# Two-layer attention encoder: the last pair's output stays in SBUF, the output projection loads two tiles ahead, and the last pair and the first transfers are reordered

## The chip, the cores and the metric

One core of one Trainium2 chip runs the whole kernel in one launch. The metric is the device time of that launch in microseconds (us), shown as the median of several runs; a separate profiled execution gives the trace.

## The reference

1088 tokens (1024 of a prompt, 64 of a sample that has 256 cached positions) go through two layers of width 1024. Cut to what matters:

```python
# layer 0: one input projection feeds two groups of 8 heads, one output projection
q_a, ckv, kr, q_b, k_b, v_b = _even_project(x, pos, w_in, g_q, w_uq, g_kv)   # latents, RMS norm, rotation
o_a = _blockwise(lambda qb, pb: _softmax_attend(qb, k_a, v_a, _chunk_mask(pb, pos), MLA_SCALE), q_a, pos)
o_b = _band_prompt(q_b, k_b, v_b, table)
y = jnp.concatenate([o_a.reshape(B, S, H_A * V_DIM), o_b.reshape(B, S, H_B * HEAD_DIM)], -1) @ w_out
# layer 1: 16 stick-breaking heads
log_1m = jnp.where(mask, jax.nn.log_sigmoid(-z), 0.0)
tail = lax.cumsum(log_1m, axis=z.ndim - 1, reverse=True) - log_1m
w = jnp.where(mask, jnp.exp(jax.nn.log_sigmoid(z) + tail), 0.0)
return o.reshape(B, S, MIX_C) @ w_out, k, v
# both layers
x = _layer_norm(ALPHA * x + mix, g1, b1)
ff = jnp.square(jax.nn.relu(x @ w_up)) @ w_down
return _layer_norm(ALPHA * x + ff, g2, b2)
```

The change touches the latents of layer 0 (`x @ w_in` for the first 1056 columns) and `y = concat(...) @ w_out` with the layer norm behind it, in both layers.

## The kernel before

Everything is fp32. A product of two fp32 matrices is done as three matmuls on TensorE (`mm3`): each operand is split into a high half H, which ScalarE writes, and a low half L = x - H, which VectorE writes (`split`); the products are H*H, H*L and L*H. So each operand passes ScalarE and VectorE before TensorE can use it. Tokens come in nine tiles of 128 (`TOK`, the last of 64).

The order of instructions on each engine is set by a planner that runs when the kernel is built, from the order in which the code issues them; TensorE, ScalarE, VectorE and GpSimd then execute their own rows in order, and all DMAs are issued in order from SyncE's queue. A row waits for the data that it reads and for the readers of the buffer that it overwrites; all behind it on the same engine waits too.

- `latents` (the start): the weight columns for the key latent (`w_ck`, four pieces), x (nine tiles, `xraw`) and the columns for the query latent (`w_ql`, eight pieces) are loaded and split; nine tiles of key latents, then nine of query latents are made. GpSimd rotates part of each key tile (`ropem`). g_q, the query constants (`qconst`, spread into a DRAM buffer `qr_d`) and the first weights of the head pairs (`w_bk`, `w_bq`, `w_bv`) are loaded here too.
- `attend`: a pair of heads has nine units (head, quarter; quarter 4 is the sample's), done in the order `self.order`. Each unit's output `o` goes to DRAM: to `oT_d`, seven blocks of 128 rows of the concatenated heads, or, for the pair that comes last (`self.late`), to `oTl_d`.
- `out_early`: while the last pair's attention still runs, w_out's eight blocks are loaded and split, and three tiles of tokens in layer 0 (`EARLY`: 0, 4, 1; four in layer 1: 0, 4, 1, 5) are multiplied with the seven blocks that are ready. `self.paced` interleaves these steps with the units.
- `out_proj`: then, in the order `OUT_ORDER`, the rest: an early tile needs only the late block's product, any other tile all eight. `operand` loads a tile's rows of `oT_d` and `oTl_d`, splits them and loads the residual. A layer norm (`norm`) follows each tile; the last two tiles run together.
- Buffers of one size, called slots, are shared by w_out, operands, residuals and results (`Slots`: `take` gives the first free one that fits, `give` puts it at the end of the list). A tile's name in a listing, as `wo0_10_2136`, is the slot (`wo0_10`) and a running number. Whoever takes a slot waits for the last reader of what was in it.

Line numbers in the profile: 138 and 139 are the two halves of `split`, 143 to 145 the matmuls of `mm3`, 161 a transpose, 304, 309 and 318 the loads of w_ck, w_ql and x, 169 the load of a weight, 607 and 609 the scans of the stick-breaking attention, 674 and 676 the products with V, 1043 and 1044 the loads of an operand.

## Time and profile before

| | |
|---|---|
| median of 3 runs | 2840.68 us (2839.82 to 2844.84) |
| profiled execution | 2842.44 us, of which 2840.6 are the span of the trace |
| mean granted TensorE clock | 0.987 |
| TensorE busy (PE) | 2737.7 us, 96% |
| VectorE (DVE), ScalarE (ACT), GpSimd (POOL) busy | 76%, 53%, 27% |
| DMA | 335.60 MB, 118 GB/s in the mean |

The page names lines of the program and tiles without their numbers: `s<-xH,wH` is a product of xH and wH into the PSUM tile s. "[1.52 <-ACT sl L138]" behind an instruction is the idle time of its engine before it, and what ended that. The chain is the row of work that ended last, followed back from the end. A window row gives, after the stretch and its length, the busy time of PE, PEld, DVE, ACT and POOL in it (with the number of instructions), the clock that was granted to TensorE, the mean busy share of the DMA engines and the GB/s moved.

### The profile page before, as it was taken

The page shows a single profiled execution, that of the slowest core. Times are in us where ns is not written, and L with a number is a line of the kernel's source. Part 1 is how long each engine was busy: PE and PEld are TensorE (multiplying, and loading weights), DVE is VectorE, ACT ScalarE, POOL GpSimd, SP SyncE. Part 2 cuts the span into 40 slices and gives each one's busy share as a digit, 9 for nine tenths or more (in the row PEclk, how much of TensorE's full clock was granted, in tenths as well). Part 3 has the DMA queues.
Part 4 walks back from the last instruction along what each step waited for, and adds up shares of the span by engine and source line. Part 5 has one row for each costly group of instructions (what it writes and reads, how often), then busy time and mean ns, then how long its engine had stood idle before and what let it go on. Part 6 is the DMA issues. An engine that isn't in the chain of part 4 may idle for free.

```text
span 2840.6 us, 46995 instructions
## 1 busy us (share of the span) xinstructions
PE 2737.7 (96%) x16907; PEld 2499.6 (88%) x16907; DVE 2160.4 (76%) x3837; ACT 1512.2 (53%) x3104; POOL 776.0 (27%) x890
## 2 busy tenths in 40 slices
PE   7999989999999999999999999998999999999998
PEld 7999978887899998878789999998879999977776
DVE  4266684885867777999978888888686777689998
ACT  4266664882555556333247777777445555543331
POOL 3123341652200002222533344344230000122235
PEclk9999999999999999999999999998999999999999
DMA  7122155334243447344231111113242444654442
GB/s 225 51 77 76 56 152 151 84 109 147 98 136 129 148 159 267 118 145 143 82 110 57 46 60 51 51 53 103 78 144 86 159 141 136 230 177 133 158 122 77
DMA packets 235752, 335.60 MB, mean 118 GB/s; under 512 B 45472, under 2 KB 168128, under 8 KB 235520
## 3 DMA queue, kind: packets, MB, share of 16 engines
q1 hardware_dynamic: 235520, 332.61, 37.2%
q8 instruction: 134, 2.20, 0.3%
q14 instruction: 98, 0.80, 0.1%
HBM read 217.83 MB, written 113.33 MB: 117 GB/s over the span
## 4 chain that ended last, share of the span: by engine, by line
PE 78%; DVE 9%; ACT 4%; DMA 4%; issue 3%; POOL 1%; SPq 0%; DVEq 0%; ACTq 0%; POOLq 0%
PE d L143 9%; PE d L144 9%; PE d L145 9%; PE s L143 5%; PE s L145 5%; PE s L144 5%; PE t L143 5%; PE t L144 5%; PE t L145 5%; PE t L161 4%; PE s L542 3%; PE pv L676 2%; PE pv L674 2%; PE pv L145 2%; PE pv L143 2%
## 5 line engine op out<-in xcount | busy, mean ns | idle before, releaser
L610 POOL TENSOR_TENSOR G<-G,S 128x384 f32<-128x384 f32 (+4 forms) x200 | 207.4, 1041 | 347.8 <-DVE S L607 128.4
L143 PE MATMUL d<-xH,wH 128*128 128x384 f32 (+1 forms) x792 | 266.4, 336 | 1.7 <-ACT kraw L509 1.6
L145 PE MATMUL d<-xH,wL 128*128 128x384 f32 (+1 forms) x792 | 264.0, 333 | 1.6 <-DVE wL L139 1.6
L144 PE MATMUL d<-xL,wH 128*128 128x384 f32 (+1 forms) x792 | 264.0, 333 | 0.0
L139 DVE TENSOR_TENSOR wtL<-t,wtH 128x512 fp32r<-128x512 f32 (+2 forms) x328 | 196.8, 618 | 54.3 <-ACT wtH L138 47.1
L138 ACT ACTIVATE wtH<-t 128x512 fp32r<-128x512 f32 (+2 forms) x328 | 170.6, 545 | 64.4 <-PE t L161 32.8
L549 POOL TENSOR_TENSOR R<-R,inv 128x640 f32<-128x640 f32 (+6 forms) x100 | 118.7, 1195 | 185.5 <-DVE inv L548 117.6
L674 PE MATMUL pv<-wtH,V 128*128 128x256 f32 (+1 forms) x624 | 159.3, 280 | 8.3 <-ACT o L634 4.0
L676 PE MATMUL pv<-wtL,V 128*128 128x256 f32 (+1 forms) x624 | 155.2, 289 | 7.0 <-DVE wtL L139 7.0
L143 PEld LDWEIGHTS d<-xH,wH 128*128 128x128 f32 x792 | 150.1, 190 | 5.4 <-ACT kraw L509 2.7
L607 DVE TENSOR_TENSOR_SCAN S<-S,own 128x513 f32<-128x513 f32 (+3 forms) x144 | 143.9, 1006 | 13.8 <-ACT S L600 12.2
L145 PEld LDWEIGHTS d<-xH,wL 128*128 128x128 f32 x792 | 149.9, 189 | 3.2 <-DVE wL L139 1.8
L144 PEld LDWEIGHTS d<-xL,wH 128*128 128x128 f32 x792 | 149.9, 189 | 1.0
L138 ACT ACTIVATE wo<-wo 128x1024 fp32r<-128x1024 f32 (+4 forms) x100 | 87.9, 883 | 113.9 <-DMA wo<-a_d 21.4
L674 PEld LDWEIGHTS pv<-wtH,V 128*128 128x128 f32 x624 | 120.1, 192 | 13.7 <-ACT o L634 6.3
L676 PEld LDWEIGHTS pv<-wtL,V 128*128 128x128 f32 x624 | 120.0, 192 | 10.8 <-DVE wtL L139 9.6
L161 PE MATMUL t<-ident,G 128*128 128x128 f32 x600 | 107.4, 282 | 12.6 <-POOL G L610 6.4
L542 PE MATMUL s<-kS,qH 128*128 128x384 f32 (+3 forms) x288 | 106.4, 372 | 4.9 <-ACT G L601 2.7
L600 ACT ACTIVATE S<-s 128x384 f32<-128x384 f32 (+4 forms) x200 | 99.1, 495 | 12.3 <-PE s L542 8.7
L601 ACT ACTIVATE G<-s 128x384 f32<-128x384 f32 (+4 forms) x200 | 100.1, 501 | 0.7 <-PE t L161 0.7
L139 DVE TENSOR_TENSOR wo<-wo,wo 128x1024 fp32r<-128x1024 f32 (+3 forms) x72 | 81.9, 1140 | 24.2 <-ACT wo L138 24.2
L542 PE MATMUL s<-kS,qL 128*128 128x384 f32 (+3 forms) x288 | 97.7, 341 | 0.0
(1724 smaller groups left out, 9836.0 us busy)
## 6 DMA issues: line engine op xcount, KB each, us to landing
wo<-a_d SPq DMA_DIRECT2D x53, 512.0 KB, 3.6
a_d<-wo SPq DMA_DIRECT2D x34, 544.0 KB, 4.2
sl<-a_d SPq DMA_DIRECT2D x29, 512.0 KB, 3.7
wo<-in_w_up SPq DMA_DIRECT2D x26, 512.0 KB, 4.1
wo<-in_w_dn SPq DMA_DIRECT2D x25, 512.0 KB, 5.4
sl<-in_w_dn SPq DMA_DIRECT2D x23, 512.0 KB, 6.3
xs<-a_d SPq DMA_DIRECT2D x19, 512.0 KB, 3.6
a_d<-sl SPq DMA_DIRECT2D x17, 544.0 KB, 5.0
```

The costliest lines, as they stand in the source:

```text
L138: self.nc.scalar.activation(H, src, AF.Copy)
L139: (engine or self.nc.vector).tensor_tensor(L, src, H.bitcast(F32), op=ALU.subtract)
L143: i = mm(out, aH, bH, start=first, stop=False)
L144: mm(out, aH, bL, start=False, stop=False)
L145: mm(out, aL, bH, start=False, stop=last)
L161: return self.nc.tensor.transpose(out, in_, self.ident[:n, :n])
L542: self.nc.tensor.matmul(ps[:, :n], q, k, start=i == 0, stop=i == len(passes) - 1)
L549: nc.gpsimd.tensor_tensor(R[:, :nk], R[:, :nk], inv.to_broadcast([P, nk]), op=ALU.mult)
L607: nc.vector.tensor_tensor_scan(s[r], s[r], own, carry, op0=ALU.mult, op1=ALU.max)
L610: nc.gpsimd.tensor_tensor(G[:, :n], G[:, :n], S[:, 1 : n + 1], op=ALU.mult)
L674: mm(out, v, wH[:, s : s + n], start=bi == 0 and s == 0, stop=False)
L676: mm(out, v, wL[:, s - n : s], start=False, stop=bi == len(banks) - 1 and j == bank[-1][0])
```

## The change

Four parts.

1. The start. `x_piece` runs two tiles ahead of the products and w_ql's pieces one tile later than before; the loads of g_q, the query constants, w_bk, w_bq and w_bv get a dependency without a wait (`after`) on a later product (`marks`), which moves them back in the planner's order.
2. The last pair of each layer has an order of units of its own (`LAST`), and its output goes by DMA from SBUF to SBUF into a slot, `late_raw`, instead of to `oTl_d`; `late_part` splits it in pieces of 256 tokens. An early tile then needs no load of its own.
3. `out_proj` loads operands ahead (`out_load` for the tile three places on, `out_operand` for the split of the one two places on, between the two halves of a tile's products). `OUT_ORDER` begins with tile 6, which is no early tile; its load stands at the start of the last early tile's step, its split at the end (`self.ahead`). g and b are loaded behind it, and `new_xq` is called there.
4. The slots are taken in another order: `out_space` adds the `wo` slots and takes `late_raw` before the five slots of the weight pool are put in the list.

How the rows move. First SyncE's queue at the start of the program (`praw` are pieces of w_ck and w_ql, `xraw` tiles of x, `wraw` weights, `qc` and `qr_d` the query constants). Before:

```order
L304 DMA praw_98<-in_w_ck 128x576
L318 DMA xraw_102<-in_xT 128x8x128
L304 DMA praw_106<-in_w_ck 128x576
L344 DMA rope_118<-in_rope_tok 128x288
L290 DMA gkv_120<-in_g_kv 128x256
L290 DMA gq_122<-in_g_q 128x768
L318 DMA xraw_181<-in_xT 128x8x128
L304 DMA praw_110<-in_w_ck 128x576
L169 DMA wraw_975<-in_w_bk 128x1024
L410 DMA qc_1363<-in_qconst 32x384
L318 DMA xraw_242<-in_xT 128x8x128
L304 DMA praw_114<-in_w_ck 128x576
```

And in the changed kernel, in the same place:

```order
L313 DMA praw_97<-in_w_ck 128x576
L327 DMA xraw_101<-in_xT 128x8x128
L313 DMA praw_105<-in_w_ck 128x576
L327 DMA xraw_117<-in_xT 128x8x128
L356 DMA rope_121<-in_rope_tok 128x288
L299 DMA gkv_123<-in_g_kv 128x256
L313 DMA praw_109<-in_w_ck 128x576
L327 DMA xraw_125<-in_xT 128x8x128
L313 DMA praw_113<-in_w_ck 128x576
L327 DMA xraw_182<-in_xT 128x8x128
L318 DMA praw_186<-in_w_ql 128x768
L327 DMA xraw_243<-in_xT 128x8x128
```

The second, third and later x tiles move ahead; g_q, w_bk and the query constants are gone from here. g_q stands at row 36 of the queue now, the constants at rows 52 to 60, w_bk, w_bq and w_bv at rows 63, 66 and 67.

Second, layer 0, where the last early tile ends and the first whole tile (6) begins: the changed kernel's ACT rows. `wo0_0_1888` is `late_raw`, `wo0_19_2161` the late block's high half, `xs0_7` the raw rows of tile 2, `wo0_1_2132` those of tile 6 and `wo0_10_2136` tile 6's high half.

```order
L646 ACTIVATE otmp_2088_8395<-pv_2083_8381 64x256
L647 ACTIVATE o_2087_8394<-pv_2083_8381 64x256
L141 ACTIVATE wo0_19_2161_8659<-wo0_0_1888_7781 128x256 x4
L141 ACTIVATE xs0_10_2199_8839<-xs0_7_2186_8766 128x896
L141 ACTIVATE wo0_10_2136_8617<-wo0_1_2132_8567 128x896
```

Behind the last output of the attention (`o_2087`) come the four pieces of the late block, one other tile's split and then tile 6's; before the change this place held a split of one 128x128 piece of the late block. The PE rows there:

```order
L146 MATMUL d_2135_8594<-wraw_2108_8438,wo0_16_2129_8562 128x512
L147 MATMUL d_2135_8594<-wH0_2109_8439,wo0_16_2129_8562 128x512
L148 MATMUL d_2135_8594<-wraw_2108_8438,wo0_19_2130_8563 128x512
L146 MATMUL s_2175_8681<-wo0_2_2090_8402,wo0_10_2136_8617 128x512
L147 MATMUL s_2175_8681<-wo0_3_2091_8403,wo0_10_2136_8617 128x512
```

The last early matmul reads slot `wo0_19`, into which the late block's high half goes next, and the row behind it already needs tile 6's high half, in slot `wo0_10`, which held the last early tile's residual until then. In layer 1 the places are alike: tile 6's first matmul follows the last early one, and on ACT four pieces of the late block and then tile 6's split stand between.

Third, VectorE in layer 1 ahead of the early products (`wo1_3`, `wo1_6` and so on, 128x1024, are low halves of w_out's blocks, `wtL` and `S` belong to the attention, 128x896 is the low half of the first early tile). Before:

```order
L139 TENSOR_TENSOR wo1_12_4919_23840<-wo1_10_4917_23837,wo1_11_4918_23839 128x1024
L139 TENSOR_TENSOR wtL_4751_23296<-t_4749_23290,wtH_4750_23295 128x512
L607 SCALAR_TENSOR_TENSOR S_4765_23355<-S_4765_23355,own_3390_16535 128x513
L139 TENSOR_TENSOR wo1_15_4922_23846<-wo1_13_4920_23843,wo1_14_4921_23845 128x1024
L607 SCALAR_TENSOR_TENSOR S_4776_23395<-S_4776_23395,own_3390_16535 128x385
L139 TENSOR_TENSOR wo1_18_4925_23852<-wo1_16_4923_23849,wo1_17_4924_23851 128x1024
L139 TENSOR_TENSOR wtL_4754_23309<-t_4752_23303,wtH_4753_23308 128x512
L139 TENSOR_TENSOR wtL_4757_23322<-t_4755_23316,wtH_4756_23321 128x512
L139 TENSOR_TENSOR wraw_4928_23858<-wo1_19_4926_23855,wo1_20_4927_23857 128x896
```

And now:

```order
L142 TENSOR_TENSOR wo1_12_4907_23831<-wo1_10_4905_23828,wo1_11_4906_23830 128x1024
L142 TENSOR_TENSOR wo1_7_4923_23863<-wL1_4920_23858,wo1_4_4922_23862 128x896
L620 SCALAR_TENSOR_TENSOR S_4785_23395<-S_4785_23395,own_3383_16529 128x385
L142 TENSOR_TENSOR wtL_4774_23352<-t_4772_23346,wtH_4773_23351 128x512
L142 TENSOR_TENSOR wo1_15_4910_23837<-wo1_13_4908_23834,wo1_14_4909_23836 128x1024
L142 TENSOR_TENSOR wo1_18_4913_23843<-wo1_16_4911_23840,wo1_17_4912_23842 128x1024
L142 TENSOR_TENSOR wtL_4777_23364<-t_4775_23359,wtH_4776_23363 128x384
L651 TENSOR_TENSOR o_4764_23321<-pv_4757_23295,o_4764_23321 64x256
L622 SCALAR_TENSOR_TENSOR S_4788_23405<-S_4788_23405,S_4785_23395 128x385
L142 TENSOR_TENSOR wraw_4916_23849<-wo1_19_4914_23846,wo1_20_4915_23848 128x1024
```

The early tile's low half (128x896) stood behind all of w_out's splits that this stretch holds; it now stands ahead of three of them.

The diff, cut to its core:

```diff
-OUT_ORDER = [[0, 5, 4, 2, 1, 6, 8, 3, 7], [0, 2, 4, 6, 1, 5, 8, 3, 7]]
+OUT_ORDER = [[6, 4, 5, 0, 2, 1, 8, 3, 7], [6, 4, 2, 0, 5, 1, 8, 3, 7]]
+LAST = [[(0, 3), (1, 1), (0, 2), (1, 0), (0, 4), (1, 3), (0, 1), (1, 2), (0, 0)],
+        [(0, 0), (1, 1), (0, 1), (1, 2), (0, 4), (1, 3), (0, 2), (0, 3), (1, 0)]]
...
+    def after(self, dma, mark):
+        if mark is not None:
+            self.tc.add_manual_dep(dma.ins, mark.ins.name, mybir.DependencyInfo(
+                mybir.DependencyClass.NoSync, mybir.DependencyReason.DATA), reason="pace")
...
+        marks = []
         ck_piece(0)
         x_piece(0)
         for k in (2, 4, 6):
             ck_piece(k)
+        x_piece(1)
         rope = self.tl(pa, [P, 9, ROPE], "rope", 1)
         nc.sync.dma_start(rope, io["rope_tok"])
         gkv = self.bcast(pa, io["g_kv"], CKV, "gkv")
-        gq = self.bcast(pa, io["g_q"], QL, "gq")
+        gq = None
 
         for t, (t0, n) in enumerate(TOK):
+            if t < 7:
+                x_piece(t + 2)
             if t:
-                x_piece(t)
-            if t < 8:
-                ql_piece(t)
+                ql_piece(t - 1)
...
+        gq = self.bcast(pa, io["g_q"], QL, "gq", marks[5])
...
-                first = self.weight(io["w_bk"][0], [P, KD, P])
+                first = self.weight(io["w_bk"][0], [P, KD, P], marks[-1])
...
-            nc.sync.dma_start(qc[:, :n], io["qconst"][:, c0 : c0 + n])
+            self.after(nc.sync.dma_start(qc[:, :n], io["qconst"][:, c0 : c0 + n]), marks[10])
...
-        return (self.oTl_d if blk == self.late else self.oT_d[blk - (blk > self.late)]), r
+        return (self.late_raw.bitcast(F32) if blk == self.late else self.oT_d[blk - (blk > self.late)]), r
...
+    def out_space(self, layer, side):
         sl = self.slots = Slots(self)
+        sl.add(f"wo{layer}", side, 21 if layer else 20, 0)
+        self.late_raw = sl.take([T], F32R)
+        self.order = LAST[layer]
         for tag in ("wraw", "wH0", "wL0", "wH1", "wL1"):
             sl.free.append((self.wp, tag, 0, D))
-        sl.add(f"wo{layer}", side, 21 if layer else 20, 0)
...
+                lhs[t] = self.out_operand(t, xres)
+                ys[t] = sl.take([D]), lhs[t].pop()
+                if t == EARLY[layer][-1]:
+                    self.ahead = self.out_load(OUT_ORDER[layer][0], xres)
...
+                    self.ahead = self.out_operand(OUT_ORDER[layer][0], xres, self.ahead)
...
+    def out_load(self, t, xres):
+        sl, (t0, n) = self.slots, TOK[t]
+        raw, xr = sl.take([KD, P]), sl.take([D])
+        self.nc.sync.dma_start(raw[:, : KD - 1, :n], self.oT_d[:, :, t0 : t0 + n].rearrange("k p t -> p k t"))
+        self.nc.sync.dma_start(xr[:n], xres[t0 : t0 + n, :])
+        return raw, xr
+    def out_operand(self, t, xres, loaded=None):
+        sl, (t0, n) = self.slots, TOK[t]
+        raw, xr = loaded or self.out_load(t, xres)
+        oH = sl.take([KD, P], F32R)
+        oL = sl.take([KD, P], F32R) if n == P else None
+        lo = oH[:, :, n:] if oL is None else oL
+        self.split(oH[:, : KD - 1, :n], lo[:, : KD - 1, :n], raw[:, : KD - 1, :n])
+        if oL is None:
+            self.split(oH[:, KD - 1, :n], lo[:, KD - 1, :n], self.late_raw[:, t0 : t0 + n].bitcast(F32))
+        sl.give(raw)
+        return [oH, oL, xr]
...
+        late = [sl.take([T], F32R), self.late_raw]
+        turned = set()
+        def late_part(t):
+            u = t // 2
+            if t < 8 and u not in turned:
+                turned.add(u)
+                c = slice(u * 2 * P, (u + 1) * 2 * P)
+                self.split(late[0][:, c], late[1][:, c], late[1][:, c].bitcast(F32))
+        loads, ops = {}, {order[0]: self.ahead}
+        def load(t):
+            if t is not None and t not in ys and t not in ops:
+                loads[t] = self.out_load(t, xres)
 
         def operand(t):
+            if t is None:
+                return
+            late_part(t)
+            if t in ys:
+                ops[t] = None, None, None
+            elif t not in ops:
+                ops[t] = self.out_operand(t, xres, loads.pop(t))
...
+        load(order[1])
+        load(order[2])
+        gb = [self.bcast(sl, io[f"ln_mix_{x}"][layer : layer + 1, :], D) for x in "gb"]
+        operand(order[0])
+        operand(order[1])
+        between[0]()
+        for j, t in enumerate(order[:-2]):
+            load(order[j + 3] if j + 3 < len(order) else None)
+            oH, oL, xr = ops[t]
+            if xr is not None:
+                ys[t] = sl.take([D])
+            early = oH is None
...
+                if h == 0:
+                    operand(order[j + 2])
```

More of the change, by code (lines that the diff above doesn't have):

```diff
@@ L1528, in do, with start @@
                 prep[c].pop(0)()
+        def start():
+            self.new_xq()
+            prep.extend(self.quadrant_sums(c) for c in range(2))
         def before():
@@ L1539, in after @@
             do(0, 1)
-        self.out_proj(layer, ws, ys, xres, xmid, (before, after))
+        self.out_proj(layer, ws, ys, xres, xmid, (start, before, after))
         plain(0, 0)
```

115 lines of the change are left out of this document (48 added, 67 removed).

## The prediction

> **What bounds the kernel now.** I read the page first, for who carries the end of the kernel. The first line is busy time by engine; the second is the share of each in the chain of work that ended last.
>
> ```profile
> PE 2737.7 (96%) x16907; PEld 2499.6 (88%) x16907; DVE 2160.4 (76%) x3837; ACT 1512.2 (53%) x3104; POOL 776.0 (27%) x890
> PE 78%; DVE 9%; ACT 4%; DMA 4%; issue 3%; POOL 1%; SPq 0%; DVEq 0%; ACTq 0%; POOLq 0%
> ```
>
> PE is busy for 2737.7 of 2840.6 us. The change neither adds nor removes a matmul (PE's matmuls in the two listings add up to the same number of columns), so all that can be won is the 2840.6 - 2737.7 = 103 us in which PE stands, and time in which it runs at half its clock. Next I read, by stretches, the three places that the change touches: the start, the step from layer 0's attention into its output projection, and the same step in layer 1. The columns are PE, PEld, DVE, ACT and POOL busy, granted clock, DMA share, GB/s.
>
> ```profile
> 20.00:30.00 10.00, 7.60 (x59) 7.36 (x58) 6.09 (x10) 6.63 (x18) 4.87 (x13) 1.00 1.07 374
> 30.00:40.00 10.00, 9.21 (x73) 8.95 (x71) 6.01 (x11) 6.88 (x19) 9.42 (x26) 1.00 0.97 278
> sum 70.00, PE 52.10 PEld 49.22 DVE 31.55 ACT 33.96 POOL 21.81; mean PE 7.44 PEld 7.03 DVE 4.51 ACT 4.85 POOL 3.12
> 660.00:670.00 10.00, 6.96 (x34) 5.22 (x32) 2.98 (x6) 1.07 (x3) 0.73 (x1) 1.00 0.44 121
> 670.00:680.00 10.00, 5.99 (x15) 4.53 (x16) 7.38 (x10) 4.54 (x6) 2.94 (x2) 0.66 1.04 327
> 1970.00:1980.00 10.00, 8.30 (x45) 6.22 (x44) 7.50 (x11) 8.53 (x19) 3.68 (x8) 0.84 0.83 295
> 1980.00:1990.00 10.00, 5.53 (x19) 3.76 (x18) 10.00 (x9) 9.42 (x18) 5.40 (x6) 0.50 0.76 248
> 1990.00:2000.00 10.00, 6.27 (x26) 5.87 (x26) 10.00 (x11) 5.04 (x10) 4.57 (x7) 0.50 0.21 69
> 2000.00:2010.00 10.00, 10.00 (x61) 8.79 (x60) 9.32 (x14) 5.05 (x14) 3.36 (x9) 0.97 0.34 97
> 2050.00:2060.00 10.00, 10.00 (x44) 7.86 (x43) 1.92 (x5) 1.37 (x2) 0.00 (x0) 1.00 0.96 300
> ```
>
> The sum row is of 0 to 70 us: PE stands 17.9 us there, all of it before 60. In 660 to 680 it stands 7.05 us, in 1970 to 2000 9.9 us, with a clock of 0.50 from 1980 on and DVE full. At 2050 to 2060, where layer 1's output projection begins, PE does not stand at all.
>
> **The start.** What PE waited for up to 62 us, and the chain in order of time:
>
> ```profile
> PE d L143 <- ACT xH L138: 7.2, 1, 7.2
> PE s L143 <- ACT xH L138: 3.3, 2, 2.7
> PE s L143 <- ACT wqlH L138: 2.9, 1, 2.9
> 6.33 8.69 DMA wraw<-in_w_bk
> 17.53 5.99 DMA wraw<-in_w_bq
> 47.08 3.90 DMA xraw<-in_xT
> 12.89 1.06 ACT L138 ACTIVATE xH<-xraw 128x1024 fp32r<-128x1024 f32 x1 [4.95 <-DMA xraw<-in_xT]
> ```
>
> PE waits for pieces of x and of the latent weights, and the chain to them runs through loads of w_bk and w_bq, which PE needs only much later. The last tile of x is issued at 47.08. The change takes gq, the query constants with their twelve stores into qr_d, w_bk, w_bq and w_bv out of this queue and puts them behind it, and moves each x tile two tiles ahead.
>
> What that can give at most: 17.9 us of standing, less the first 7.2 us, which stay (the first products still need the same first piece of w_ck and of x), leaves 10.7 us. To it come matmuls at half clock. In the next rows one of 288 columns follows the one before after 0.24 us until 17.3 us, and after 0.13 us then; some 22 of them, 0.11 us each, are 2.4 us.
>
> ```profile
> 9.14 0.44 PE L144 MATMUL d<-wckL,xH 128*128 128x288 f32 x1
> 9.38 0.44 PE L145 MATMUL d<-wckH,xL 128*128 128x288 f32 x1
> 17.71 0.29 PE L143 MATMUL s<-wckH,xH 128*128 128x288 f32 x1
> 17.84 0.29 PE L144 MATMUL d<-wckL,xH 128*128 128x288 f32 x1
> ```
>
> So 13 us is the ceiling. How much of it is reached follows from the loads. Per tile the new queue brings 524 KB of x and 393 KB of w_ql, 917 KB; at the 278 to 374 GB/s of the rows that takes 2.5 to 3.3 us, and the 24 matmuls of a tile at 0.13 us take 3.1 us. Loads and products are about even, so small waits stay, and POOL's chain for the key's rotation (9.42 of 10 us busy in 30 to 40) is not shortened. By bytes, w_bk, w_bq and w_bv (0.52 MB each), gq (0.39 MB) and the qr_d stores (12 of up to 0.20 MB) are 4.3 MB, 11.5 us at 374 GB/s, which agrees with the ceiling. I take 9 us, 4 to 12. Below 4 it would need POOL or the load of the last tile of x to hold PE as now. The work that was moved back costs nothing where it goes: after 60 us PE is full and the queues are nearly idle, and the first product with w_bk comes at 130 us:
>
> ```profile
> 100.00:110.00 10.00, 10.00 (x62) 9.97 (x61) 2.48 (x6) 2.04 (x6) 0.55 (x1) 1.00 0.14 39
> L143 PE MATMUL s<-xH,wH x32: 306/334/426, 130.8 to 159.3; 128*128 128x384 f32 x24, 128*128 128x320 f32 x8
> ```
>
> If this cover were gone, a weight would be late by its load and split, 6 to 9 us by the two rows of the chain.
>
> **Layer 0, entry into the output projection.** The last early tile's products are issued up to 665 us; then:
>
> ```profile
> 666.81 0.51 PE L143 MATMUL s<-wo,sl 128*128 128x512 f32 x1 [1.52 <-ACT sl L138]
> 674.01 0.79 PE L143 MATMUL s<-wH,xs 128*128 128x512 f32 x1 [5.53 <-ACT xs L138]
> 679.30 0.60 PE L143 MATMUL s<-wo,xs 128*128 128x512 f32 x1
> 679.73 0.41 PE L144 MATMUL s<-wo,xs 128*128 128x512 f32 x1
> 666.47 6.36 DMA xs<-oTl_d
> 672.91 1.06 ACT L138 ACTIVATE xs<-xs 128x1024 fp32r<-128x1024 f32 x1 [0.46 <-DMA xs<-oTl_d]
> ```
>
> First 1.52 us for the late block's reload, then 5.53 us for the first whole tile, whose load is issued only now, and behind that 13 matmuls at 0.43 us where 0.23 is normal, 2.6 us. Together 9.7 us. The change removes the reload, loads tile 6 before the last early tile and issues g and b behind. But it does not remove the stall. In the order of instructions (above, in the part on the change) tile 6's high half is written into the slot that held the residual of the last early tile, and the late block's high half into the slot of that tile's low half, which PE reads until its last early matmul. So behind that matmul ACT must do four late pieces of 128x256, then the next tile's split (it is ahead on the same queue), then tile 6's split, and only then does PE go on. Prices, from groups of the same shape:
>
> ```profile
> L138 ACT ACTIVATE wtH<-t 128x256 fp32r<-128x256 f32 x16 | 6.0, 378 | 6.4 <-PE pv L674 5.5 <-PE t L161 0.4 <-PE pv L691 0.4
> L138 ACT ACTIVATE wo<-wo 128x896 fp32r<-128x896 f32 x5 | 4.8, 957 | 1.7 <-DVE wH L1021 1.5 <-DMA wo<-oT_d 0.2
> ```
>
> 4 x 0.38 + 2 x 0.96 = 3.4 us, and 0.2 us of signals: 3.6. Whether half clock follows such a gap lies between two rows: behind 1.52 us the matmuls kept 0.23 us, behind 5.53 us they lost 2.6; I take 2. New loss 5.6, gain 9.7 - 5.6 = 4 us; bounds 1 (2.6 us lost and 2 us more, if the raw tile or the split ahead of it is late) and 9.7 (no stall). The Trainium skill ("TensorE: Matmul & The Clock Gate", Part 1) gives a window of about 3.4 us that runs freely, and half the clock after an idle one. By that rule 3.6 us of idle need not fill a window, the penalty could be nothing and the gain 6 us; no row here shows a gap of 3.6 us. The new order of the last pair's units does not change when the early products can start here, and one more split of w_out falls into that stretch, about 1 us of ACT, which I put within the bounds.
>
> **Layer 1.** The stretch before the early products:
>
> ```profile
> PE pv L676 <- DVE wtL L139: 4.2, 2, 3.2
> PE t L161 <- POOL G L610: 3.8, 2, 2.4
> 1991.50 1.20 DVE L139 TENSOR_TENSOR wo<-wo,wo 128x1024 fp32r<-128x1024 f32 x1
> 1992.62 1.84 DVE L607 TENSOR_TENSOR_SCAN S<-S,own 128x385 f32<-128x385 f32 x1
> 1996.70 1.08 DVE L139 TENSOR_TENSOR wraw<-wo,wo 128x896 fp32r<-128x896 f32 x1
> 2000.10 0.94 DVE L607 TENSOR_TENSOR_SCAN S<-S,own 128x385 f32<-128x385 f32 x1
> 2001.39 0.48 PE L143 MATMUL d<-wH,wo 128*128 128x512 f32 x1
> ```
>
> DVE is the bound: seven splits of w_out, the first tile's split, scans and attention splits stand in one row, and the first early product (2001.39) gives PE work of its own. Before, the first tile's low half comes behind all seven w_out splits; after, behind four or five, with the rest behind it. Between them and now one finds two splits of 1.2 us less, about two scans of 0.94 to 1.84 less and one attention split of about 0.6, so the first early product can start about 6 us earlier, at 1995, or a little more. But it needs the last weight blocks within its 21 matmuls (4.8 us at 0.23), and these two or three splits come only 4 to 7 us behind. Of some 21 us lost from 1971 to 2001 (9.9 standing, the rest at half clock) I take 7 as won, 0 to 12. Here the range is widest: the scans, 0.94 us alone and 1.84 us beside a busy POOL, make DVE's sum uncertain by some microseconds.
>
> At the projection's start the same new wait comes, where now there is none (10.00 of 10 us busy): four late pieces and tile 6's split, 4 x 0.38 + 0.96 + 0.2 = 2.7 us, and 0 to 2.6 us of half clock, of which I take 1.5. Sum for layer 1: 7 - 4.2 = 3 us, from -5 to 10.
>
> **The sum.** 9 + 4 + 3 = 16 us. The profiled execution took 2842.4 us (span 2840.6 and 1.8 around it), 1.8 us over the median of the runs, 2840.7. So 2826.4 for a profiled execution, and 2825 us as a median.
>
> **Rivals.** About 0.2% (5.7 us) is what a measurement can tell from no change, so "faster" ends at 2835.
>
> Everything removed: the start reaches 12, the split at layer 0 hides behind the early products (9.7), and in layer 1 the stretch gives 12 at no new wait. 34 us, 2807. For it: nothing but slots ties the splits, and PE has 4.8 us of products there. Against it: the order binds both high halves to slots that the last early matmul or the add behind it frees. Half of this (one of the stalls really gone) is 2815. Chance of either 0.17.
>
> The start gives little: POOL's rotation chain, 9.42 of 10 us busy in 30 to 40, or the in-order transposes behind it hold PE as the loads do now. 4 us instead of 9, and the rest 4 to 5 in all: 2840.7 - 8.5 = 2832. For it: PE also waits there for more than loads. Against: of the 10.7 us, 6.2 (3.3 and 2.9) are waits for splits of loaded pieces. Chance 0.22.
>
> It does not do what it says: "made ready early" is a load ahead and no split ahead, and a wait as long as today's stands at both entries. Layer 0 then gives 0, layer 1 -2, the start 4: 2839, no change. Chance 0.10.
>
> Slower: in layer 1 the small gaps keep PE at half clock. From 1980 to 2000 the granted clock is 0.50 with PE about 60% busy; the early products pulled forward wait for single weight splits, so the gaps are spread over a longer time. Each further microsecond of such a stretch loses half a microsecond; against the 13 us of the other parts it decides from 26 us on, and for a measurable loss from 38 us on, so the slow stretch would run to about 2040 instead of 2002: 2847. For it: the clock stayed at 0.50 through busy pieces of several microseconds. Against: from 2000 to 2010, with the first early products, the clock was back at 0.97. The Trainium skill ("TensorE: Matmul & The Clock Gate", Part 1) says that one busy window of about 3.4 us brings the full clock, which speaks against 38 us; the trace agrees there (0.97). Chance 0.05.
>
> **How the numbers follow.** Forecast 0.46; both sorts of full removal 0.17; little at the start 0.22; not as it says 0.10; slower 0.05. Faster by over 0.2%: 0.46 + 0.17 + 0.22 = 0.85; within: 0.10; slower 0.05. The likeliest alone spans 2819 to 2832 (the start 6 to 11, each layer 3 either way, added as squares). For 8 in 10 the range goes from 2810, between the two full removals, to 2836.
>
> **What would show it.** Start: PE's busy time in 0 to 60 at 50 to 52 us, no wait of over 1 us behind x after the first, w_bk's load issued past 50 us. Layer 0: one wait of 3 to 4 us in front of the first product of tile 6, its releaser ACT's split, in place of 1.52 and 5.53. Layer 1: the first early product about 1995 less what the start and layer 0 gave, and a wait of 2 to 3 us at the first product of tile 6, where there was none. The forecast is wrong if tile 6's products follow without a wait, if a wait for POOL appears in 20 to 45 us, or if the granted clock after 1975 stays at 0.50 for over 30 us.

## The result, and the profile after

The change makes the kernel slower: 2853.74 us (median of 11 runs, 2848.63 to 2861.45) against 2842.72 us for the kernel before in the same sessions (11 runs, 2839.16 to 2848.85). The ratio is 1.0039, 95% interval 1.0028 to 1.005, so 11 us lost where 16 were forecast as won. The profiled execution took 2858.17 us (span 2856.4), 15.7 us more than the profiled one of before. Engines and stretches of the changed kernel, columns as in the prediction:

```profile
PE 2743.6 (96%) x16907; PEld 2507.0 (88%) x16907; DVE 2158.5 (76%) x3840; ACT 1512.1 (53%) x3107; POOL 787.5 (28%) x890
0.00:50.00 50.00, 38.72 (x258) 36.77 (x259) 25.54 (x40) 27.58 (x67) 22.13 (x66) 1.00 0.78 235
50.00:100.00 50.00, 50.00 (x300) 49.27 (x299) 11.68 (x26) 14.35 (x41) 4.24 (x11) 1.00 0.52 125
670.00:680.00 10.00, 7.56 (x34) 5.91 (x32) 2.72 (x6) 1.33 (x4) 0.60 (x1) 1.00 0.95 294
680.00:690.00 10.00, 5.94 (x16) 4.74 (x17) 3.47 (x4) 1.79 (x2) 0.00 (x0) 0.66 0.94 215
```

The start is better, and the entry into layer 0's output projection still stands. That doesn't say where the loss is. Since both traces hold the same matmuls, I lined them up by work: columns of matmul done so far, at 0.235 us per 512, here called C (it runs from 0 to 2581). At equal C the difference of the two clocks tells how far one kernel is behind, and its steps tell where it fell behind:

```
C            what stands there                  step, us   forecast
0-50         start                                -7.4      -9
325-375      layer 0, first branch's last pair   +11.4       0
500-525      layer 0, second branch's last pair   +7.0       0
525-600      its projection, first whole tile     -1.5      -4
1300-1325    last norm of layer 0, entry layer 1  +7.9       0
1750-1775    layer 1, last pair                   -7.1      -7
1775-1925    layer 1, projection                  +4.8      +4.2
the rest                                          +0.6
sum                                              +15.7     -15.8
```

The two rows of layer 1 are largely the profiled execution of before: kernels whose layer 1 is that of before (e1, e7, e15, e16 below) show -2.2 to -3.5 in the first of them and +2.2 to +5.8 in the second. In the other named rows, kernels that have the code of before there stay within 1.5 us of it. Kernels with one and the same changed code can differ more: those with the new start have +7.5 (e5) to +11.4 at C 325-375.

So the forecast terms came out roughly, and three places for which it had no term cost 26 us. Here are their rows after the change, PE and who held it. First the first branch's last pair (L141 and L142 are the two halves of a split now, L146 to L148 the matmuls, L164 a transpose):

```profile
404.81 0.44 PE L146 MATMUL d<-qnH,wH 128*128 128x384 f32 x1 [2.95 <-ACT x L823]
427.03 0.69 PE L146 MATMUL d<-qnH,wH 128*128 128x384 f32 x1 [5.33 <-DVE raw L142]
425.90 0.49 ACT L141 ACTIVATE raw<-d 128x384 fp32r<-128x384 f32 x1 [7.94 <-DMA qr_d<-raw]
```

PE waits 5.33 us for a piece of the next branch's query, and ScalarE's split of it waits 7.94 us for the buffer `raw` to be stored. Before the change those two rows read as follows, so this wait makes 3.3 of the 11.4 us; the rest lies in smaller waits and in matmuls at half clock:

```profile
423.89 0.49 ACT L138 ACTIVATE raw<-d 128x384 fp32r<-128x384 f32 x1 [3.84 <-DMA qr_d<-raw]
425.03 0.44 PE L143 MATMUL d<-qnH,wH 128*128 128x384 f32 x1 [2.00 <-DVE raw L139]
```

Then layer 0's second last pair, at its early products:

```profile
624.58 0.58 PE L687 MATMUL pv<-wtH,V 128*128 128x256 f32 x1 [2.47 <-ACT o L647]
630.27 0.48 PE L146 MATMUL s<-wo,wo 128*128 128x512 f32 x1 [1.15 <-DVE nm L598]
636.46 0.80 PE L148 MATMUL s<-wo,wo 128*128 128x512 f32 x1 [2.37 <-DVE wo L142]
632.37 4.03 DVE L142 TENSOR_TENSOR wo<-wo,wo 128x896 fp32r<-128x896 f32 x1
631.93 3.52 POOL L562 TENSOR_TENSOR R<-R,inv 128x896 f32<-128x896 f32 x2
```

Before, the first early product stood at 624.31 and the split of this shape took 1.07 us:

```profile
624.31 0.50 PE L143 MATMUL s<-wH,wraw 128*128 128x512 f32 x1 [0.29 <-ACT wraw L138]
626.91 1.07 DVE L139 TENSOR_TENSOR wH<-wo,wraw 128x896 fp32r<-128x896 f32 x1
```

Third, the step into layer 1, where the first key weight's split stands behind the last norm:

```profile
1469.28 1.37 PE L164 MATMUL t<-ident,wo 64*128 64x64 f32 x8 [5.15 <-issue]
1469.84 1.39 DVE L284 SCALAR_TENSOR_TENSOR sl<-sl,mv,wH 128x512 f32<-128x512 f32 x2
1471.26 1.06 ACT L141 ACTIVATE wH<-wraw 128x1024 fp32r<-128x1024 f32 x1 [0.30 <-DVE sl L284]
```

Before, that split was done 47 us earlier and the norm's vector stood in another slot (`wo`):

```profile
1424.22 1.06 ACT L138 ACTIVATE wH<-wraw 128x1024 fp32r<-128x1024 f32 x1 [1.74 <-DMA wraw<-in_w_ck]
1460.02 1.41 DVE L275 SCALAR_TENSOR_TENSOR wo<-wo,mv,wo 128x512 f32<-128x512 f32 x2
```

### The profile page after: what moved, and what is told of

Its sections match the earlier page's. It is cut to its first block, busy times and chain, and to the rows that moved or that the text cites. A ratio compares the mean times of both kernels' runs of the same rounds, so it can differ in the third digit from the quotient of the medians.

```text
span 2856.4 us, 46990 instructions
## 1 busy us (share of the span) xinstructions
PE 2743.6 (96%) x16907; PEld 2507.0 (88%) x16907; DVE 2158.5 (76%) x3840; ACT 1512.1 (53%) x3107; POOL 787.5 (28%) x890
## 5 line engine op out<-in xcount | busy, mean ns | idle before, releaser
L623 POOL TENSOR_TENSOR G<-G,S 128x384 f32<-128x384 f32 (+4 forms) x200 | 214.8, 1079 | 342.6 <-DVE S L620 138.9
L146 PE MATMUL d<-xH,wH 128*128 128x384 f32 (+1 forms) x792 | 267.4, 338 | 1.5 <-ACT kraw L522 1.4
L148 PE MATMUL d<-xH,wL 128*128 128x384 f32 (+1 forms) x792 | 263.1, 332 | 0.0
L142 DVE TENSOR_TENSOR wtL<-t,wtH 128x512 fp32r<-128x512 f32 (+2 forms) x328 | 196.4, 617 | 57.0 <-ACT wtH L141 53.0
L141 ACT ACTIVATE wtH<-t 128x512 fp32r<-128x512 f32 (+2 forms) x328 | 170.2, 545 | 58.7 <-PE t L164 40.8
L146 PEld LDWEIGHTS d<-xH,wH 128*128 128x128 f32 x792 | 150.6, 190 | 5.0 <-ACT kraw L522 2.2
L148 PEld LDWEIGHTS d<-xH,wL 128*128 128x128 f32 x792 | 150.3, 190 | 1.3
L141 ACT ACTIVATE wo<-wo 128x1024 fp32r<-128x1024 f32 (+4 forms) x107 | 91.1, 868 | 110.1 <-DMA wo<-a_d 22.5
L164 PE MATMUL t<-ident,G 128*128 128x128 f32 x600 | 104.9, 277 | 15.5 <-POOL G L623 9.0
L142 DVE TENSOR_TENSOR wo<-wo,wo 128x1024 fp32r<-128x1024 f32 (+4 forms) x81 | 89.5, 1119 | 17.8 <-ACT wo L141 17.7
L141 ACT ACTIVATE wo<-sl 128x1024 fp32r<-128x1024 f32 (+3 forms) x65 | 58.8, 907 | 82.2 <-PE pv L147 13.5
```

Of the source, the lines that this page charges most:

```text
L141: self.nc.scalar.activation(H, src, AF.Copy)
L142: (engine or self.nc.vector).tensor_tensor(L, src, H.bitcast(F32), op=ALU.subtract)
L146: i = mm(out, aH, bH, start=first, stop=False)
L148: mm(out, aL, bH, start=False, stop=last)
L164: return self.nc.tensor.transpose(out, in_, self.ident[:n, :n])
L623: nc.gpsimd.tensor_tensor(G[:, :n], G[:, :n], S[:, 1 : n + 1], op=ALU.mult)
```

## The experiments

Each time stands beside the kernel before on the same chip (2842.7 to 2845.9 us); "step" is a step of the table above, measured against the profiled execution of before.

**Which part of the change costs what.** The new start alone (`latents` as changed, all else as before):

> The kernel before with the reordered first transfers alone. In the two traces the start gained 7.4 us, and between 379 and 450 us 11 us were lost. Theory A: this loss comes from the start itself, whose shifted order changes how the stores into qr_d and the units of the last band pair meet; then this kernel takes 2842.7 - 7 + 11 = about 2846, and its trace shows both steps. Theory B: the loss comes from the other parts (the sample unit's two stores in place of one); then it takes about 2835 and the trace shows the first step only.

2846.75 us, ratio 1.0011 (1.0002 to 1.002). Steps: -8.8 at the start, +11.2 at C 325-375, at most 1.4 in any other row of layer 0 or at the step into layer 1. So the first loss belongs to the start, though it stands some 300 us behind it. The opposite, the changed kernel with the old start:

> The changed kernel with the old start. Theory A (the 11 us between 379 and 450 belong to the start): 2853.7 + 7 - 11 = about 2850, no step there. Theory B (they belong to the other parts): 2853.7 + 7 = about 2861, with the step. In both the step of 7 us in layer 0's last pair, that of 9 us at layer 1's first product and the gain of 7 us in layer 1's last pair stay.

2853.82 us, 1.0039 (1.0026 to 1.0052). No step at C 325-375 (-0.1); +7.3 at the second last pair and +7.5 into layer 1 stay. And the parts in layer 1 alone, layer 0 and the start as before:

> The kernel before, with the change in layer 1 alone (order of the last pair, its output on chip, loads ahead, slots), the start and layer 0 as before. Theory A: the 8 us before layer 1's first product come from what the change did to layer 0's slots, so they are not there; the last pair wins 7 us, the entry of the projection loses 4 to 5: 2843 - 3 = 2840. Rival: the loss before layer 1's first product comes with layer 1's own code: 2848.

2844.65 us, 1.0001 (0.9993 to 1.001), with -0.1 at the step into layer 1. So that step comes from layer 0's parts, and layer 1's own parts are worth nothing that can be measured. Of them, the new order of the last pair's units alone:

```diff
+                self.order = [(0, 0), (1, 1), (0, 1), (1, 2), (0, 4), (1, 3), (0, 2), (0, 3), (1, 0)]
```

> The kernel before, with nothing but layer 1's last pair in the new order of units. Theory A: the 7 us that layer 1's last pair won come from this order, which lets the first early tile's split stand ahead of three of w_out's; then this takes 2843 - 7 = about 2836 and all else stays. Rival: they come from the other order of the slots; then it takes 2843.

2847.13 us, 1.0015 (1.0006 to 1.0024): no gain. Its -2.6 in the last pair is what kernels with an untouched layer 1 show too.

**The start: order or time?** Only the loads moved back, x not loaded further ahead:

> The kernel before with one half of the new start: g_q, the query constants and the first weights moved back, x and w_ql loaded in the old order. On VectorE its rows from 180 us on are those of the whole new start. Theory A: the loss near 380 to 430 us comes from this other order of rows, however much the start has won; then the start gains 3 to 6 us, the band pair loses 8 to 11 all the same: 2846 to 2850. Theory B: that stretch ends when something ends that does not move with the start, so it takes back what the start gave and no more: 2843.

2847.3 us, 1.0016 (1.0008 to 1.0025): -7.6 at the start and +9.2 at C 325-375. The marks alone bring most of the gain, and a loss within the spread of the whole one. In all these kernels VectorE's rows differ from the kernel before from about the 150th on. Two kernels tell a changed order from a mere earlier arrival. One moves a single load, g_q:

```diff
-        gq = self.bcast(pa, io["g_q"], QL, "gq")
+        gq = None
...
+        gq = self.bcast(pa, io["g_q"], QL, "gq", marks[5])
```

> The kernel before with one load moved back: the broadcast of g_q behind the sixth product group. VectorE's row changes from about row 150 on as in the whole new start. Theory (the +11 at the first branch's last pair is that re-planned row order): the start gains 1 to 4 us, the stretch at column-time 325 to 375 loses 9 to 11 as before, and the kernel is slower than before by 5 to 9 us: 2848 to 2852. Rival (the stretch has a fixed end, and an earlier arrival is absorbed there): the stretch loses no more than the start has gained, and the time is that of before, 2843, within 2 us.

2854.88 us, 1.0029 (1.0018 to 1.0041). The start gains nothing (+0.7), and the step at C 325-375 is +10.9. One load, moved by itself, re-plans the rows: VectorE's from the 150th to the 700th are those of the changed kernel, one for one. The other kernel takes parts of the new start that leave VectorE's rows from the 150th on as they were (w_bq and w_bv are moved back too, not shown):

```diff
         for t, (t0, n) in enumerate(TOK):
-            if t:
-                x_piece(t)
             if t < 8:
+                x_piece(t + 1)
                 ql_piece(t)
...
+                first = self.weight(io["w_bk"][0], [P, KD, P], marks[6])
...
+            self.after(nc.sync.dma_start(qc[:, :n], io["qconst"][:, c0 : c0 + n]), marks[10])
```

> The kernel before with those parts of a new start that leave the rows of VectorE and ScalarE from row 150 on as they were: x one tile further ahead, the first key weight of the first branch behind the seventh product group, the q constants and the later weights moved back, g_q where it was. Theory (row order): the start gains 4 to 8 us, the stretch at column-time 325 to 375 loses nothing (under 2), and the kernel is faster than before by 4 to 8 us: 2835 to 2839. Rival (an earlier arrival is absorbed at a fixed end): the stretch gives back what the start gained, and the time is 2842 to 2846.

2840.45 us, 0.998 (0.9971 to 0.999): -3.8 at the start, +0.3 at C 325-375. It is faster than the kernel before, by 0.2%. Rows of these two, e15 first; what ScalarE waits for is the same wait, 7.24 us in the one and 4.04 in the other:

```profile
432.60 0.49 ACT L138 ACTIVATE raw<-d 128x384 fp32r<-128x384 f32 x1 [7.24 <-DMA qr_d<-raw]
433.73 0.44 PE L143 MATMUL d<-qnH,wH 128*128 128x384 f32 x1 [3.29 <-DVE raw L139]
```

```profile
422.06 0.49 ACT L138 ACTIVATE raw<-d 128x384 fp32r<-128x384 f32 x1 [4.04 <-DMA qr_d<-raw]
423.19 0.45 PE L143 MATMUL d<-qnH,wH 128*128 128x384 f32 x1 [2.20 <-DVE raw L139]
```

So the order, not the time of arrival, costs the 11 us. How it does is not shown: PE's wait for `raw` is only 1.1 us longer in e15 than in e16, and which of the moved rows costs how much was not separated.

**Layer 0's last pair: the slots.** The changed kernel with the weight pool's five slots ahead of the `wo` slots again:

```diff
+        for tag in ("wraw", "wH0", "wL0", "wH1", "wL1"):
+            sl.free.append((self.wp, tag, 0, D))
         sl.add(f"wo{layer}", side, 21 if layer else 20, 0)
         self.late_raw = sl.take([T], F32R)
         self.order = LAST[layer]
-        for tag in ("wraw", "wH0", "wL0", "wH1", "wL1"):
-            sl.free.append((self.wp, tag, 0, D))
```

> The changed kernel with the weight pool's five slots ahead of the others in the list again, so that two blocks of w_out are split before layer 0's last pair, as before. Theory A: the 7 us lost in layer 0's last pair come from the w_out splits in VectorE's row there; two fewer give back 4 to 7 us, 2848. Rival: they come from the new order of the pair's units; no change, 2854. The 9 us at layer 1's first product stay in both, since the slot of its first weight is still held by a late tile there.

2863.26 us, 1.0071 (1.0059 to 1.0084). The step at C 500-525 is gone (-0.1 for +7.0). The first early tile's low half, on which the early products wait, comes 7.7 us earlier than in the changed kernel (632.37) and takes 1.08 us instead of 4.03:

```profile
624.67 1.08 DVE L142 TENSOR_TENSOR wo<-wraw,wo 128x896 fp32r<-128x896 f32 x1
```

It stands behind five splits of w_out on VectorE there, in the changed kernel behind all seven, of which the first comes 6.4 us later (e4 first, then the changed kernel; before the change there were seven too, from 606.00 on):

```profile
610.70 1.21 DVE L142 TENSOR_TENSOR wo<-wH,wL 128x1024 fp32r<-128x1024 f32 x1
617.11 1.22 DVE L142 TENSOR_TENSOR wo<-wo,wo 128x1024 fp32r<-128x1024 f32 x1
```

As a time it is a miss all the same, for the step into layer 1 is +13.2 and layer 1's projection +8.0: the slots go round from here on, and other tiles end up in other slots.

**The first whole tile.** In the prediction the stall came from four late pieces and two splits. The changed kernel's rows:

```profile
677.60 1.33 ACT L141 ACTIVATE wo<-wo 128x256 fp32r<-128x256 f32 x4 [7.86 <-PE d L148]
682.22 0.95 ACT L141 ACTIVATE xs<-xs 128x896 fp32r<-128x896 f32 x1 [3.29 <-DMA xs<-oT_d]
683.08 0.93 ACT L141 ACTIVATE wo<-wo 128x896 fp32r<-128x896 f32 x1
684.06 0.80 PE L146 MATMUL s<-wo,wo 128*128 128x512 f32 x1 [6.50 <-ACT wo L141]
```

The three splits took what was forecast (1.33, 0.95, 0.93), but the middle one waits 3.29 us for its own load. First guess, the load of the tile two places on takes the queue; it was issued later:

```diff
-        load(order[2])
...
+                    if j == 0:
+                        load(order[2])
```

> The changed kernel, but the third tile's load is issued in the middle of the first tile's products and no more ahead of them. Theory A: in layer 0 TensorE stood 6.5 us before the first whole tile because ScalarE had the split of another tile, whose load was not there, ahead of that tile's; then the wait falls to about 2.7 us (four late pieces and one split) and with less half clock 4 to 5 us are won: 2849. Rival: the slots that come free late hold it; the wait stays at 6 us, 2854.

2855.79 us, 1.0043 (1.003 to 1.0056), and PE's wait was 6.24 us. A miss: the tile whose split stands ahead is another one, tile 2, while the load that was issued later is tile 5's. So tile 2's split and the late pieces were ordered behind tile 6's, by a dependency without a wait (`behind` is built like `after`; `turned` is tile 6's high split):

```diff
-    def split(self, H, L, src, engine=None):
-        self.nc.scalar.activation(H, src, AF.Copy)
+    def split(self, H, L, src, engine=None, row=None):
+        i = self.nc.scalar.activation(H, src, AF.Copy)
+        self.behind(i, row)
...
                     self.ahead = self.out_operand(OUT_ORDER[layer][0], xres, self.ahead)
+                    self.row = self.turned
```

> The changed kernel, with one difference in the order of ScalarE's row at the entry to each output projection: the split of the tile that runs first stands ahead of the late pieces' splits and of the split of the tile whose load is still on its way. Theory (the 6.50 us wait before the first high-half product of layer 0 is a row order: 1.33 us of late pieces, 3.29 us of waiting for the second tile's load and 0.95 us of its split all stand ahead of the 0.93 us split that the product needs): the wait falls from 6.50 to about 2 us (DVE's last addition 0.7, the split 0.93, signals), the half clock behind it shrinks too, and the time falls by 5 to 7 us, to about 2848. In layer 1 the wait falls from 2.26 to about 1.9. Rival (the wait is held by the split's own input or by the slots that the tile uses): the wait stays at about 6 us and the time at 2854.

2848.45 us, 1.0019 (1.0011 to 1.0028), 5.3 below the changed kernel; step -7.7 for -1.5. The wait, as forecast here, is under 2 us:

```profile
672.17 2.18 ACT L141 ACTIVATE wo<-wo 128x896 fp32r<-128x896 f32 x5 [8.56 <-DVE wL L1047]
673.17 0.50 PE L148 MATMUL s<-wo,wo 128*128 128x512 f32 x1 [1.76 <-ACT wo L141]
```

The five instructions on ScalarE are tile 6's split and the four late pieces, in this order now. (In this kernel L148 to L150 are the matmuls; in e14 and e18 below, L143 and L144 are the halves of a split and L166 a transpose.) In layer 1 the wait fell from 2.26 to 1.76 us, about as forecast.

**The step into layer 1.** The last norm's vectors g and b, and where they stood, by the listing of the rows:

```
kernel      ln_ffn_g   ln_ffn_b   step at C 1300-1325
before      wo0_14     wo0_18       (0)
changed     wH0        wH1         +7.9
e5          wH1        xs0_8      +13.3
e14         xs0_8      xs0_10     +10.7
e18         sl0_0      wo0_8       +0.8
```

wH0 and wH1 receive the high halves of layer 1's first weights. The first theory was that these and the splits of x wait in one row. e5 kept the norm, its vectors and its accumulators (not shown), out of the first weight's slots (`wraw`, `wH0`, `wL0`):

```diff
+            if not last:
+                sl.keep = ("wraw", "wH0", "wL0")
             g = self.bcast(sl, io["ln_ffn_g"][layer : layer + 1, :], D)
             b = self.bcast(sl, io["ln_ffn_b"][layer : layer + 1, :], D)
+            sl.keep = ()
```

> The changed kernel, but layer 0's last norm (its g, b and its nine accumulators) takes none of the three slots into which layer 1's first weight is loaded and split. Theory A: the 9 us lost before layer 1's first product are the wait of that load and split for the last norm's readers; they go, 2845. Rival: they come from the order in which the transposes of the last tiles stand; then they stay, 2854.

2862.32 us, 1.0063 (1.005 to 1.0077), step +13.3: a miss. e11 also moved the next two weights' loads back:

```diff
-                self.weight(w[kind][pair], [P, KD, P], sooner)
+                self.weight(w[kind][pair], [P, KD, P], sooner if kind != "k" else None)
...
+                self.seam = self.transpose(tp[:, j, :n], y[:n, c : c + P])
...
+                                ..., 0, sooner=None if pair else self.seam)
```

> The changed kernel, with layer 0's last norm kept out of the slots of layer 1's first weight, as in the run of that alone, and in addition layer 1's first query and value weights marked to load behind the last transposes of x. Theory (the step of 8 us at the start of layer 1 is ScalarE's row: the split of a weight that is still loading stands ahead of the splits of x, once because the first weight has to wait for its slot, and, with that mended, because a second weight's split is put there): with both out of the way the step from layer 0 to layer 1 is at most 2 us instead of 7.9 (13.3 in the run with the slots alone), and the time is 2846 to 2849. Rival (the stretch is bound by the norm's transposes and signals, whatever the weights do): the step stays at 8 us or more and the time at 2854 or more.

2856.82 us, 1.0052 (1.0038 to 1.0066), step +10.4: another. e14 kept the three slots free through the whole last group of the down projection:

> The changed kernel, with the three slots of layer 1's first key weight kept free from the last group of layer 0's down projection on (before, only from its norm on, which left the step at +13). No mark on the later weights. Theory (the load of that weight waits because the low half of the last down-projection operand stands in its landing slot until the last product of layer 0, and ScalarE's row then stands still for the weight's split): the load moves ahead of the eight stores of x, its split ahead of the splits of x, and the step from layer 0 to layer 1 falls from 7.9 us to at most 2, so the time falls from 2854 to 2846 to 2849. Rival (the norms and the transposes of x bound that stretch, whatever the weight does): the step stays at 8 or more and the time at 2854 or more.

2858.45 us, 1.0038 (1.0026 to 1.0051). Load and split of the weight were out of the way at last, and the step was still +10.7. Its rows show what was left:

```profile
1449.52 1.06 ACT L143 ACTIVATE wH<-wraw 128x1024 fp32r<-128x1024 f32 x1 [3.67 <-PE s L149]
1456.41 1.41 DVE L287 SCALAR_TENSOR_TENSOR wo<-wo,rr,xs 128x512 f32<-128x512 f32 x2
1458.76 3.47 PE L166 MATMUL t<-ident,wo 128*128 128x128 f32 x15 [9.05 <-DVE xL L144]
```

The norm reads its vectors from `xs` until 1457.8, and PE waits 9.05 us until the first splits of x follow that. `xs` is the pool on the right, released there, and layer 1's x is put into its space. Both vectors lie where the first low half of x (`xL`) goes, which may not be written until the last norm has read them. Each of these repairs had pushed the vectors from one bad place into another. e18 is e14 with the vectors in the left pools:

```diff
-        t = pool.take([n]) if tag is None else self.tl(pool, [P, n], tag, 1)
+        t = pool.take([n], where=0) if tag is None else self.tl(pool, [P, n], tag, 1)
```

> The changed kernel with the first weight's slots of layer 1 kept free through the last group of layer 0, as in the run before of that name, and with the last norm's two vectors (ln_ffn_g, ln_ffn_b) put into slots of the pool on the left, which layer 1's x does not reuse. Theory (the step at the start of layer 1 is the place of these two vectors: in the changed kernel they hold slots of the first weights until the last norm is done, in the runs meant to mend that they held the space of the next layer's x): the splits of x run between the norms as before the change, the step from layer 0 to layer 1 falls from 7.9 (10.65 in the run before) to at most 2, and the time falls to 2846 to 2849. Rival (something else binds that stretch): the step stays at 8 or more and the time at 2854 or more.

2848.59 us, 1.0017 (1.0008 to 1.0027), 5.2 below the changed kernel; step +0.8 for +7.9. The splits of x and the norms alternate again (`neg` is the norm's step on ScalarE), and PE is full where e14, whose row stands last, had it busy for 1.25 us of 10:

```profile
1443.23 1.15 ACT L279 ACTIVATE wo<-wo,neg 128x1024 f32<-128x1024 f32 x1 [3.35 <-DVE neg L278]
1445.50 1.09 ACT L143 ACTIVATE xH<-t 128x512 fp32r<-128x512 f32 x2 [1.13 <-PE t L166]
1450.00:1460.00 10.00, 10.00 (x54) 7.93 (x53) 9.80 (x16) 4.58 (x7) 5.39 (x3) 1.00 0.21 83
```

```profile
1450.00:1460.00 10.00, 1.25 (x6) 1.27 (x7) 9.67 (x17) 2.15 (x5) 1.84 (x2) 0.65 0.53 184
```

**Do the terms add?** First e11's repair, e4's slots and e10's row order together, with the new start (e12) and with the old one (e13):

> The changed kernel with the three repairs together: the output weight's slots taken ahead of the last pair's as before the change, the norm and the weights at the start of layer 1 as in the run of the seam, and the first tile's split ahead in ScalarE's row. If the terms add: start -8, the stretch of the first branch's last pair +9 to +11, layer 0's last pair 0, layer 0's first tile -6, the start of layer 1 0 to +2, layer 1 0 to -3; sum -8 to +2, time 2836 to 2845 beside 2843 for the kernel before. Rival (each repair shifts the planner's order elsewhere, as the slots' old order did with +13 us at the start of layer 1): a new step of 5 us or more stands somewhere behind column-time 500, and the time is 2850 or more.

> The kernel of the three repairs with the old start of the program. The start and what follows from it are worth +3 us as measured alone (-8 at the start, +11 at the first branch's last pair), so if the terms add, this is about 3 us faster than the three repairs with the new start: about 2836 to 2842, 0.1 to 0.3 per cent below the kernel before. Rival (the repairs do not carry over when the start is re-planned): no difference from the other, or slower.

2856.79 us, 1.0043 (1.0031 to 1.0056), and 2855.85 us, 1.0048 (1.0035 to 1.0061). Both are misses. They carry the unmended step into layer 1 (+11.1, +10.6) and about +10 in layer 1's projection, where e4, with the same old slots beside the changed code, has +8.0. Kernels with the changed layer 1 and the new slot order have +0.3 to +6.2 there: beside the rest of the change, the old slot order is good in layer 0 and bad in layer 1. e17 put e16's start and e14's slots in place:

> All repairs together: the start of e16, the output weight's slots taken as before the change, the first tile's split ahead in ScalarE's row, the first weight's slots of layer 1 kept free through the last group of layer 0. If the terms add: start -4 to -8, first branch 0, layer 0's last pair 0, layer 0's first tile -6.5, start of layer 1 0 to +2, layer 1 0 to +3; sum -4 to -14, time 2829 to 2839 beside 2843 for the kernel before. Rival (each repair shifts the planner's order elsewhere): a new step of 4 us or more behind column-time 500, and the time is 2840 or more.

2847.98 us, 1.0006 (0.9997 to 1.0015): +9.2 into layer 1 and +10.1 in the projection, the same two, so a miss too. With e18's place for the vectors and the old slot order in layer 0 alone:

> All repairs together, second try: the start of e16, the old slot order in layer 0 only (in layer 1 it cost 5 to 9 us in the three runs that had it there), the first tile's split ahead in ScalarE's row, the last norm's two vectors in the left pool and the first weight's slots kept free. If the terms add: start -4, first branch 0, layer 0's last pair 0, its first tile -7, start of layer 1 0 to +2, layer 1 0 to -3; sum -9 to -14 against the kernel before, a ratio of 0.995 to 0.997, about 2830 to 2836. Rival (another shift of the planner's order): a new step of 4 us or more behind column-time 500 and a ratio of 0.998 or more.

2835.4 us (8 runs, 2828.93 to 2841.03) against 2842.96: 0.9969 (0.9958 to 0.9981). It beats both kernels, 7.6 us below the one before. Steps: start -6.2, first branch about 0, last pair -0.2, first whole tile -5.9, C 600-1300 +2.0, into layer 1 +1.5, layer 1's last pair and projection -0.9 together.

## Why the prediction was wrong

- **The start** was right: -7.4 and -8.8 for -9 (4 to 12). The two waits for split pieces (3.3 and 2.9 us) are gone from the list of waits; the key's nine tiles now hold PE (VectorE's `cat`, which itself waits 7.9 us for GpSimd there), so PE is busy for 48.7 us of the first 60, under the 50 to 52 that were to show it:

```profile
PE d L146 <- ACT xH L141: 7.3, 1, 7.3
PE t L164 <- DVE cat L373: 3.5, 4, 1.4
```

- **"The work that was moved back costs nothing where it goes"** is the step that failed first, and by the most, 11 us. The cover that it named (PE full after 60 us, w_bk needed at 130) was there. What it left out is that a moved load changes the planner's rows behind it, here from VectorE's 150th on, and with them a tight place at 380 to 450 us that has nothing to do with the moved load. e15 (no gain, +10.9) and e16 (gain, +0.3) show it.
- **"The new order of the last pair's units does not change when the early products can start"** in layer 0 failed by 7 us, and not through the units' order. Part 4 of the change, the order of the slots, had no term at all: with the `wo` slots taken first, the splits of w_out begin 6.4 us later, and the first early tile's low half behind them comes 7.7 us later and beside GpSimd. e4 takes the 7 us away and leaves the units' order in place.
- **The first whole tile** was the right mechanism and the wrong size: 3.6 us of wait forecast, 6.50 measured; the half clock behind it cost about 2.2 us for the 2 of the sum. The three terms of the wait were right; the bound "if the split ahead of it is late" was what happened (3.29 us). Gain 1.5 for 4.
- **The step into layer 1** was no term and no rival. I followed the slots only where the change names them. They are one list for all of a layer, and the two vectors of its last norm took what the list gave 800 us later. That this place was the cause is shown by e18; e5, e11 and e14 were mended only in part.
- **Layer 1** was about right in its places (-7.1 for -7, +4.8 for +4.2; the wait at tile 6 2.26 us for 2.7). But kernels that leave layer 1 alone show -2.2 to -3.5 and +2.2 to +5.8 in these rows, so that the two sums agree so well is in part luck, and the measured worth is nothing (e9) instead of 3 us. The slower rival, a clock at one half in layer 1 to 2040 us, did not occur.

Sum: 7.4, 1.5 and about 0 us were won, 9 where 16 were forecast; 11.4, 7.0 and 7.9 were lost where there was no term. All three losses are orders that follow from the change, two of slots and one of rows, and two of them stand far behind the code that it touches. The signs of being wrong that the prediction named lay all in places for which it had a term, and none of them came up.

## What to carry to other kernels

Where a planner sets the rows and buffers go round in one list, a local edit can have a remote price. Where to look for it can be read before a run, though not how much it is: compare the rows of both kernels far behind the edit, and ask for each buffer that now stands elsewhere who next needs that space. Line the two traces up by work done, not by time; the steps then name the places. And when a repair misses, look whether it moved the same tile into another bad place before giving up the cause.

## What the runs showed of the hardware

A split on VectorE that reads two SBUF tiles took 4.03 us beside two GpSimd instructions of 3.52 us together, 1.07 before the change. It ended at 636.40, 0.95 us after GpSimd's end at 635.45, as if VectorE had stood until the other was through. The Trainium skill ("SBUF — State Buffer", Who interferes with whom) says that a VectorE instruction with two SBUF inputs contends with a GpSimd instruction that reads SBUF, over a shared pair of ports that is an exclusive lock; the trace agrees (4.03 against 1.07, and 0.95 behind GpSimd's end).

PE at half clock followed a gap of 2.26 us in a stretch that was full before it (layer 1, tile 6): matmuls of 512 columns came 0.43 us apart from 2074.94 to 2077.93 instead of 0.23, some 1.5 us lost, as much as the prediction's sum had behind a wait of 2.7. Behind 1.76 us (e10) none did. Behind 2.37 us (at 636.46, above) they did from 637.05 to 640.89, but there PE had worked for only 0.4 of the 3.3 us before. The Trainium skill ("TensorE: Matmul & The Clock Gate", Part 1) has the clock follow a free-running window of about 3.4 us; here a gap of two thirds of it was enough. So the prediction's doubt whether 3.6 us must cost anything was not borne out. Rows of the changed kernel:

```profile
637.05 0.63 PE L146 MATMUL s<-wo,wo 128*128 128x512 f32 x1
637.47 0.63 PE L147 MATMUL s<-wo,wo 128*128 128x512 f32 x1
2074.08 0.50 PE L146 MATMUL s<-wo,wH 128*128 128x512 f32 x1 [2.26 <-ACT wH L141]
2074.94 0.63 PE L147 MATMUL d<-wo,wH 128*128 128x512 f32 x1
2075.36 0.63 PE L146 MATMUL s<-wL,wo 128*128 128x512 f32 x1
```
